# Two weight tiles split inside the opening of a hybrid decoder block, and two gate tiles moved ahead of the compression tiles

## The chip, the cores and the metric

One core of a Trainium2 chip runs the whole program. The metric is the device time of one execution in microseconds (us), as the median of several runs. The names of the engines are those of the profile: PE (TensorE, matrix products), DVE (VectorE), ACT (ScalarE), POOL (GpSimd) and SP (SyncE, which here issues nearly all loads).

## The reference, cut to what matters

The program computes one decoder layer on 512 tokens of width 1024. The input is normed, modulated, and projected by one wide matrix; its columns feed three token mixers (A, B and C) and three gates.

```python
ada = (cond @ ada_w[l] + ada_b[l])[:, None, :]
sh1, sc1, gt1, sh2, sc2, gt2 = jnp.split(ada, 6, axis=-1)
h = modulate(rmsnorm(x, norm1_w[l]), sh1, sc1)
p = h @ w_in[l]
p_a, p_b, p_c, p_gate = split_cols(p, IN_GROUPS)
y_a = hgrn2_mixer(*split_cols(p_a, A_SPLITS), ...)      # gated linear recurrence
y_b = nsa_mixer(*split_cols(p_b, B_SPLITS), ...)        # compressed / selected / window attention
y_c = rwkv7_mixer(p_c, ...)                             # delta rule; p_c is first mixed with its shifted self
ga, gb, gc = jnp.split(jax.nn.sigmoid(p_gate), 3, axis=-1)
merged = ga * (y_a @ w_branch[l, 0]) + gb * (y_b @ w_branch[l, 1]) + gc * (y_c @ w_branch[l, 2])
x = x + gt1 * (merged @ w_out[l])
h = modulate(rmsnorm(x, norm2_w[l]), sh2, sc2)
x = x + gt2 * ((jax.nn.silu(h @ ffn_w1[l]) * (h @ ffn_w3[l])) @ ffn_w2[l])
return rmsnorm(x, final_norm_w)
```

## The kernel before

Every large product is made in three matrix products of reduced-precision halves. A weight tile (128 columns of `w_in`, 128x1024 floats in the buffer `wraw`, of which there are three) is loaded by SP. ACT casts it to its high half `whi`, DVE subtracts to get its low half `wlo` (two buffers each), and PE then multiplies `whi` with `hhi`, `whi` with `hlo` and `wlo` with `hhi` for each of eight slices of the inner dimension, 24 matmuls in all, into an accumulator of a ring. The rings are called "g", "f", "m" and "n" and have two accumulators each; the trace names the products by the ring.

The opening is scheduled by the compiler's own list scheduler. `first_gemm` (line 579) makes the modulated input `h` slice by slice and multiplies each slice at once with six column tiles of mixer C, whose accumulators are two of "m", "g" and "f". The loop of line 608 takes the six in the order 0 to 5. Then `c_setup` (line 723) reads the six accumulators through `c_shift`: ACT scales, DVE adds the row shifted by one token. It begins with the two "m" accumulators (`lora` and `xg`, with a tanh and a sigmoid), then takes the "g" and "f" ones, which frees them.

From line 1614 on comes the counted phase (`manual_schedule`): instructions keep the order in which the program emits them, and the program picks that order by counting estimated times. `order.job` is the list of weight tiles; `order.chain` adds the mixers' step chains ("C", "pre", "A"), the conditioning sums ("D") and the bias table ("bias"). The function `tend` (line 292) loads up to three tiles ahead and splits only the first of the list, and only when all that it needs is done. `Weights` is one tile with its load, its split and its steps. The first two of the list are the query and the forget tile of head 0 of mixer A (`af("q", 0)`, `af("f", 0)`). Towards the end of the list stand eight compression tiles `kt` of mixer B, whose raw weights are used unsplit (they hold a `wraw` buffer until their products have run), and eight gate tiles `gt`. These write `merged`, which lies in the pool `pm`; that pool is opened when chain "A" is through. After the compression tiles the chain "K" (`b_compress`) makes the compressed keys and values in small steps; the attention's preparation and `b_mixer` follow, with the branch products as filling work for PE.

In the listing, `self.bproj` holds the query buffer "bq" from the start. `b_bias` (line 1213) uses it for a row of its table, and `yc` and `ya` are the two "y" buffers for the outputs of mixers C and A.

Of the kernel before, what the change touches and what calls it, by code (L numbers as in the profile page):

```python
# [17 lines left out]
P = 128  # L18
T = 512
D = 1024  # L20
KT = 8
# [82 lines left out]
class Clock:  # L104


    def __init__(self):
        self.at = dict.fromkeys(("PE", "DVE", "ACT", "POOL", "SP"), 0.0)
        self.wrote, self.read, self.slots, self.seen, self.by = {}, {}, {}, {}, {}
        self.bus, self.func, self.last, self.held = 0.0, None, 0.0, 0.0  # L110
# [97 lines left out]
class Order:  # L208
# [83 lines left out]
    def tend(self):  # L292

        loaded = sum(w.raw is not None and (w.w is None or w.split is None) for w in self.tiles)
        loaded += bool(self.steps and self.tile.split is None)
        for x, w in enumerate(self.tiles[:4]):
            if w.raw is None:
                if loaded >= 3:
                    break
                w.prepare(self.clock, 0)  # L300
                loaded += 1

        for x, w in enumerate(self.tiles[:3]):
            if all(n in self.done for n in w.needs):
                if x and self.tiles[0].hi is None:
                    self.tiles.insert(0, self.tiles.pop(x))
                break
        if self.tiles and all(n in self.done for n in self.tiles[0].needs):
            self.tiles[0].prepare(self.clock, 1)

    def job_ready(self):
# [43 lines left out]
class Weights:  # L355


    def __init__(self, load, split, steps, needs=(), ring="g"):
        self.load, self.split, self.todo, self.needs, self.ring = load, split, steps, needs, ring
        self.raw = self.w = self.hi = None  # L360

    def prepare(self, clock, split):
# [22 lines left out]
class Trunk:  # L385
# [193 lines left out]
    def first_gemm(self, xs, pool):  # L579

        nc, V = self.nc, self.nc.vector
        h = self.h
        s1 = self.t(self.cp, [P, 8], "s1")
        offs = (1536, 1664, 512, 640, 0, 1024)
        pss = [self.psm(), self.psm(), self.psg(), self.psf(), self.psg(), self.psf()]
        pa, px = self.psn(), self.psn()

        def ada(k):
            if k not in self.first_a:
                return  # L590
            aw, n = self.first_a[k]
            acc = self.t(pool, [P, 2, 2, P], "facc", bufs=2)[:, :, :n]
            for kk in range(KT):
                self.ada_sum(acc, kk, aw[:, :, kk])
            for x in range(n):
                self.ada_cols(pa[:, 2 * (k + x):2 * (k + x) + 2], [acc[:, 0, x], acc[:, 1, x]], k + x, 8)
            V.scalar_tensor_tensor(s1[:, k:k + n], self.adaT[:, 8 + k:8 + k + n], 1.0, self.vec("norm1_w", k, n), op0=ALU.add, op1=ALU.mult)

        def products(ks):
            w = []  # L600
            for k in ks:
                raw = self.first_w[k]
                whi = self.t(self.wp, [P, 1024], "whi", F32R, bufs=2)
                wlo = self.t(self.wp, [P, 1024], "wlo", F32R, bufs=2)
                nc.scalar.copy(whi[:, :768], raw[:, :768])
                V.tensor_tensor(wlo[:, :768], raw[:, :768], whi[:, :768].bitcast(F32), op=ALU.subtract)
                w.append((whi, wlo))
            for q in range(6):
                qs = slice(q * P, (q + 1) * P)
                for k, (whi, wlo) in zip(ks, w):  # L610
                    self.mm3(pss[q], (whi[:, qs], wlo[:, qs]), (h[0][:, k], h[1][:, k]), k == 0, k == KT - 1)

        ada(0)
        ada(1)
        self.modulate(xs, 0, px, h, s1[:, 0:1], self.adaT[:, 0:1], pool)
        for k in range(KT):
            if k + 2 < KT:
                ada(k + 2)
            if k + 1 < KT:
                self.modulate(xs, k + 1, px, h, s1[:, k + 1:k + 2], self.adaT[:, k + 1:k + 2], pool)  # L620
            if k != KT - 2:
                products((k,) if k < KT - 1 else (k - 1, k))
        return h, dict(zip(offs, pss))
# [73 lines left out]
        nc.vector.tensor_tensor(lo[:, :f], raw[:, :f], hi[:, :f].bitcast(F32), op=ALU.subtract)  # L697
        return tuple(x[:, :f].rearrange("p (k n) -> p k n", k=nk) for x in (hi, lo))

    def full(self, src, h, end, needs=()):  # L700

        st = []

        def steps(w):
            def step(k):
                if k == 0:
                    st.append(self.psg())
                self.mm3(st[0], (w[0][:, k], w[1][:, k]), (h[0][:, k], h[1][:, k]), k == 0, k == KT - 1)
                if k == KT - 1:
                    end(st[0])  # L710

            return [lambda k=k: step(k) for k in range(KT)]

        return Weights(lambda: self.load_w(src, KT, P), lambda raw, hi: self.cut_w(raw, hi, KT, P), steps, needs)

    def proj(self, off, h, tag, n=128):
        ps = self.psum(tag)
# [5 lines left out]
    def c_setup(self, first):  # L723

        nc = self.nc
        self.ck = {}
        lora = self.lora = self.c_shift(first.pop(1536), 12, "lora")
        nc.scalar.activation(lora[:64], lora[:64], AF.Tanh)
        xg = self.xg = self.c_shift(first.pop(1664), 13, "xg")
        nc.scalar.activation(xg, xg, AF.Sigmoid)  # L730
        for off, j, tag, bufs in ((512, 4, "k", 2), (0, 0, "r", 1), (1024, 8, "v", 2), (640, 5, "k", 2)):
            self.ck[off] = self.c_shift(first.pop(off), j, tag, bufs)

    def c_shift(self, ps, j, tag, bufs=1):
        nc = self.nc
# [398 lines left out]
    def a_mixer(self, y):  # L1134
# [3 lines left out]
        for hd in range(4):  # L1138
# [66 lines left out]
            for i in range(4):  # L1205
                tr(ps[:, i * P:(i + 1) * P], yo[:, i], self.ident)
            nw = self.vec("hgrn_norm_w", hd)
            nc.scalar.activation(y[:, hd], ps, AF.Identity, scale=nw)
            done[f"A{hd}"] = self.order.at
            yield "now"  # L1210


    def b_bias(self, qT, vg):

        nc = self.nc
        vg, qT = (x.rearrange("p a b -> p (a b)") for x in (vg, qT))
        rb, oh, row = vg[:33, TOEP:TOEP + 8], vg[:33, :TOEP], qT[:8, :TOEP]
        nc.gpsimd.memset(rb, NEG)
        nc.sync.dma_start(rb[:32], self.i["rel_bias"])
        nc.sync.dma_start(oh, self.i["onehot"])  # L1220
        yield rb, oh, ":n"
        for c0, n in ((0, 512), (512, TOEP - 512)):
            ps = self.psn()
            self.mm(ps[:8, :n], rb, oh[:, c0:c0 + n], start=True, stop=True)
            nc.vector.tensor_copy(row[:, c0:c0 + n], ps[:8, :n])
        yield row
        d = self.t(self.dr, [8, TOEP], "toep8")
        nc.sync.dma_start(d, row)
        yield 20.0
        self.b_spread(d)  # L1230
# [7 lines left out]
    def b_tiles(self, h):  # L1238
# [11 lines left out]
            return self.full(w_in[:, B_OFF + off:B_OFF + off + 128], h, end)  # L1250


        qT = self.t(pool, [P, 4, T], "bq")

        def query(i):
            src = [w_in[:, B_OFF + 256 * g + 64 * i:B_OFF + 256 * g + 64 * i + 64] for g in range(2)]
            return self.full(src, h, lambda ps: nc.scalar.mul(qT[:, i], ps, 0.125))

        vg = self.t(pool, [P, 4, 280], "bvg")
        gt = self.t(pool, [P, 4, 24], "bgt")  # L1260
# [19 lines left out]

            return Weights(lambda: self.load_w(src, 2, 280), lambda raw, hi: self.cut_w(raw, hi, 2, 280), steps, (), None)

        self.bproj = qT, kT, vg, gt
        return {**{nm: key(nm, off) for nm, off in (("kc", 512), ("vc", 640), ("ks", 768), ("kw", 1024))},
                "q": [query(i) for i in range(4)], "v": [value(kq) for kq in range(4)]}

# [232 lines left out]
    def gate_tiles(self, b, h):  # L1519

        def tile(m):
            off = G_OFF + 1024 * b + 128 * m

            def end(ps):
                self.nc.scalar.activation(self.merged[:, m], ps, AF.Sigmoid)

            return self.full(self.i["w_in"][0, :, off:off + 128], h, end, ("pm",))

        return [tile(m) for m in range(8)]

# [33 lines left out]
    def run(self):  # L1564
# [10 lines left out]
        with tc.tile_pool(name="p0", bufs=1) as p0:  # L1575
# [29 lines left out]
            self.turn_vecs(vrows[0])  # L1605
            h, first = self.first_gemm(xs, p0)
            self.turn_vecs(vrows[1])
        self.pc = pcs.enter_context(tc.tile_pool(name="pc", bufs=1))
        with tc.using_default_side("right"):
            self.pa = pas.enter_context(tc.tile_pool(name="pa", bufs=1))  # L1610
        yc, ya = self.new_y(), self.new_y()
        order = self.order
        self.cp_, self.a_ = {}, {}
        with tc.manual_schedule():
# [6 lines left out]
            order.chain("D", self.ada_steps(), 5, None)  # L1621

            bt = self.b_tiles(h)
            order.chain("bias", self.b_bias(self.bproj[0], self.bproj[2]), 6, None)
            av = lambda n, *x: self.a_pair_tiles(A_OFF + 1024 + 256 * n, h, "av", AF.Identity, f"av{n}", x)
            sg = lambda n, *x: self.a_pair_tiles(A_OFF + 1536 + 256 * n, h, "asg", AF.Sigmoid, f"sg{n}", x)
            af = lambda nm, hd, *x: self.a_tile(nm, hd, h, x)
            cr = lambda nm, p, *x: self.c_tile(nm, p, h, x)
            order.job(af("q", 0), af("f", 0), *av(0), cr("r", 1, "b0"), cr("v", 1), *sg(0), af("q", 1, "qd0"), af("f", 1, "fd0"),
                      cr("k", 2, "g0"), bt["kc"], bt["vc"], af("q", 2, "qd1"), cr("r", 2, "b1"), cr("v", 2, "G0"), af("f", 2, "fd1"),  # L1630
                      *av(1, "A1"), *sg(1, "A1"), bt["ks"], af("q", 3, "qd2"), bt["kw"], cr("k", 3, "g1"), af("f", 3, "fd2"),
                      cr("r", 3, "b2"), cr("v", 3, "G1"), *bt["q"], *bt["v"])
            kt, gt = self.b_compress_tiles(), self.gate_tiles(0, h)
            order.job(*gt[:2], *[x for n in range(4) for x in (kt[2 * n], kt[2 * n + 1], gt[2 + n])], *gt[6:])
            order.run("A")
            self.dump("ya", ya)
            pas.close()
            pks = ExitStack()
# [189 lines left out]
```

## Time and profile before

| what | us |
|---|---|
| median of 3 runs | 1171.03 (1169.71 to 1173.94) |
| the profiled execution's own time | 1174.54 |
| its span, first to last instruction | 1172.6 |
| PE busy | 1120.2 |
| DVE busy | 656.4 |
| ACT busy | 412.0 |
| POOL busy | 82.7 |

The span is what the profile shows; the execution's own time has a little around it. Matmuls overlap in the profile, so a busy PE is not a PE at its peak; the pitch from start to start tells more than the duration of one. Times in the rows are counted from the span's start. The bracket at the end of a timeline row is the idle time of the engine before that instruction and what ended it.

### The profile page before, as it was taken

The page shows a single profiled execution, that of the slowest core. Times are in us where ns is not written, and L with a number is a line of the kernel's source. Part 1 is how long each engine was busy: PE and PEld are TensorE (multiplying, and loading weights), DVE is VectorE, ACT ScalarE, POOL GpSimd, SP SyncE. Part 2 cuts the span into 40 slices and gives each one's busy share as a digit, 9 for nine tenths or more (in the row PEclk, how much of TensorE's full clock was granted, in tenths as well). Part 3 has the DMA queues.
Part 4 walks back from the last instruction along what each step waited for, and adds up shares of the span by engine and source line. Part 5 has one row for each costly group of instructions (what it writes and reads, how often), then busy time and mean ns, then how long its engine had stood idle before and what let it go on. Part 6 is the DMA issues. An engine that isn't in the chain of part 4 may idle for free.

```text
span 1172.6 us, 18592 instructions
## 1 busy us (share of the span) xinstructions
PE 1120.2 (96%) x7497; PEld 912.0 (78%) x7497; DVE 656.4 (56%) x1396; ACT 412.0 (35%) x737; POOL 82.7 (7%) x96
## 2 busy tenths in 40 slices
PE   3989999999999999899999989998999999999997
PEld 3759887878887887577878758887888888888886
DVE  5858666666757766377666745446343343432533
ACT  4352421242332231155454654435232322322221
POOL 1001010120111000110112002110000000000000
PEclk9989999999999999889999999999999999999999
DMA  9934532324243244643222105542233333333231
GB/s 284 257 105 143 131 97 73 84 67 141 57 111 82 71 118 117 194 147 99 73 63 76 33 1 148 155 137 78 85 90 100 98 90 108 90 94 104 90 108 72
DMA packets 183086, 125.28 MB, mean 107 GB/s; under 512 B 27929, under 2 KB 163111, under 8 KB 183000
## 3 DMA queue, kind: packets, MB, share of 16 engines
q1 hardware_dynamic: 182424, 123.04, 37.0%
q8 instruction: 59, 0.97, 0.3%
q10 hardware_dynamic: 576, 1.05, 0.2%
q14 instruction: 27, 0.22, 0.1%
HBM read 121.15 MB, written 5.53 MB: 108 GB/s over the span
## 4 chain that ended last, share of the span: by engine, by line
PE 86%; DVE 4%; DMA 4%; SPq 2%; ACT 2%; issue 2%; POOL 0%; POOLq 0%; DVEq 0%; ACTq 0%
PE g L438 27%; PE f L438 27%; PE m L438 18%; PE n L438 11%; SPq L191 2%; PE n L442 2%; DMA adaw<-in_ada_w_dram 1%; DMA fw<-in_w_in_dram 1%; DMA wraw<-in_w_in_dram 1%; DVE wlo L191 1%; DMA x<-in_x_dram 1%; PE m L442 1%; ACT bpt L191 0%; DVE adacc L191 0%; DVE ylo L191 0%
## 5 line engine op out<-in xcount | busy, mean ns | idle before, releaser
L191 DVE TENSOR_TENSOR wlo<-wraw,whi 128x1024 fp32r<-128x1024 f32 (+2 forms) x144 | 164.1, 1139 | 158.3 <-ACT whi L191 156.5
L191 ACT CAST whi<-wraw 128x1024 fp32r<-128x1024 f32 (+2 forms) x144 | 139.1, 967 | 282.8 <-PE f L438 119.6
L438 PE MATMUL g<-hhi,whi 128*128 128x512 f32 x360 | 155.5, 432 | 9.6 <-ACT whi L191 9.6
L438 PE MATMUL g<-hhi,wlo 128*128 128x512 f32 x360 | 143.6, 399 | 1.9 <-DVE wlo L191 1.8
L438 PE MATMUL g<-hlo,whi 128*128 128x512 f32 x360 | 143.3, 398 | 0.0
L438 PEld LDWEIGHTS g<-hhi,whi 128*128 128x128 f32 x360 | 69.8, 194 | 29.5 <-ACT whi L191 10.9
L438 PE MATMUL f<-hhi,whi 128*128 128x512 f32 x232 | 91.8, 396 | 0.0
L438 PE MATMUL f<-hhi,wlo 128*128 128x512 f32 x232 | 90.9, 392 | 0.0
L438 PE MATMUL f<-hlo,whi 128*128 128x512 f32 x232 | 90.6, 390 | 0.0
L438 PEld LDWEIGHTS g<-hhi,wlo 128*128 128x128 f32 x360 | 69.0, 192 | 20.1 <-DVE wlo L191 4.7
L438 PEld LDWEIGHTS g<-hlo,whi 128*128 128x128 f32 x360 | 69.4, 193 | 11.4 <-issue 0.5
L191 DVE SCALAR_TENSOR_TENSOR adacc<-adaw,cond,adacc 128x512 f32<-128x512 f32 x56 | 42.5, 759 | 15.6 <-DMA adaw<-in_ada_w_dram 15.0
L438 PEld LDWEIGHTS f<-hhi,whi 128*128 128x128 f32 x232 | 44.3, 191 | 8.9
L438 PEld LDWEIGHTS f<-hhi,wlo 128*128 128x128 f32 x232 | 43.6, 188 | 9.0
L438 PEld LDWEIGHTS f<-hlo,whi 128*128 128x128 f32 x232 | 43.6, 188 | 8.5
L438 PE MATMUL f<-whi,hhi 128*128 128x256 f32 (+1 forms) x144 | 44.4, 308 | 0.0
L191 DVE CUSTOM_DVE_ANT_0 bs<-m,bW 128x128 f32<-128x128 f32 (+3 forms) x64 | 30.1, 486 | 24.5 <-PE m L438 15.3
L438 PE MATMUL f<-whi,hlo 128*128 128x256 f32 (+1 forms) x144 | 41.6, 289 | 0.0
L438 PE MATMUL f<-wlo,hhi 128*128 128x256 f32 (+1 forms) x144 | 41.5, 288 | 0.0
L438 PE MATMUL f<-yhi,whi 128*128 128x512 f32 x96 | 38.8, 404 | 2.2 <-ACT yhi L191 1.4
L191 ACT ACTIVATE bs<-bs,bst 128x128 f32<-128x128 f32 (+3 forms) x64 | 35.9, 563 | 12.9 <-DVE bst L191 12.4
L191 POOL TENSOR_TENSOR merged<-merged,msg 128x512 f32<-128x512 f32 x16 | 25.9, 1622 | 202.4 <-DVE msg L191 194.5
(439 smaller groups left out, 2376.8 us busy)
## 6 DMA issues: line engine op xcount, KB each, us to landing
wraw<-in_ffn_w_dram SPq DMA_DIRECT2D x66, 512.0 KB
wraw<-in_w_in_dram SPq DMA_DIRECT2D x52, 512.0 KB
adaw<-in_ada_w_dram SPq DMA_DIRECT2D x64, 256.0 KB
aw<-in_ada_w_dram SPq DMA_DIRECT2D x16, 512.0 KB
wraw<-in_w_branch_dram SPq DMA_DIRECT2D x16, 256.0 KB
wraw<-in_w_out_dram SPq DMA_DIRECT2D x8, 512.0 KB
fw<-in_w_in_dram SPq DMA_DIRECT2D x24, 128.0 KB
toep<-toep SPq DMA_DIRECT2D x8, 320.0 KB
```

The costliest lines, as they stand in the source:

```text
L191: r = f(*a, **kw)
L438: return self.nc.tensor.matmul(o, l, r, **kw)
L442: return self.nc.tensor.transpose(o, x, ident)
```

## The change

Two tiles are split in the opening. After `first_gemm` the program now loads and splits the first two tiles of the job list into `held`, with the query buffer "bq" and one "y" buffer as the place for their halves; the two `Weights` are handed these when the job list is made. The query buffer itself, the bias table's row and `ya` are therefore allocated later, and the bias chain first waits for the mark `qA0`, set when the first tile has ended. `first_gemm` takes the two "g" tiles first, and `c_setup` reads these two first. The flag `early` lets `tend` split the first gate tile before `pm` is open. In the job list four gate tiles, not two, stand ahead of the compression tiles, and after the last pair of them one gate is left instead of three.

```diff
-        if self.tiles and all(n in self.done for n in self.tiles[0].needs):
+        if self.tiles and (self.tiles[0].early or all(n in self.done for n in self.tiles[0].needs)):
             self.tiles[0].prepare(self.clock, 1)
...
-            for q in range(6):
+            for q in (2, 4, 0, 1, 3, 5):
...
-        lora = self.lora = self.c_shift(first.pop(1536), 12, "lora")
-        nc.scalar.activation(lora[:64], lora[:64], AF.Tanh)
-        xg = self.xg = self.c_shift(first.pop(1664), 13, "xg")
-        nc.scalar.activation(xg, xg, AF.Sigmoid)
-        for off, j, tag, bufs in ((512, 4, "k", 2), (0, 0, "r", 1), (1024, 8, "v", 2), (640, 5, "k", 2)):
-            self.ck[off] = self.c_shift(first.pop(off), j, tag, bufs)
+        for off, j, tag, bufs in ((512, 4, "k", 2), (0, 0, "r", 1), (1536, 12, "lora", 1), (1664, 13, "xg", 1), (640, 5, "k", 2), (1024, 8, "v", 2)):
+            o = self.ck[off] = self.c_shift(first.pop(off), j, tag, bufs)
+            if off == 1664:
+                lora, xg = self.lora, self.xg = self.ck.pop(1536), self.ck.pop(1664)
+                nc.scalar.activation(lora[:64], lora[:64], AF.Tanh)
+                nc.scalar.activation(xg, xg, AF.Sigmoid)
...
-            nc.scalar.activation(y[:, hd], ps, AF.Identity, scale=nw)
+            if hd == 0:
+                y.append(self.new_y())
+            nc.scalar.activation(y[0][:, hd], ps, AF.Identity, scale=nw)
...
-        rb, oh, row = vg[:33, TOEP:TOEP + 8], vg[:33, :TOEP], qT[:8, :TOEP]
+        vg = vg.rearrange("p a b -> p (a b)")
+        yield "qA0"
+        rb, oh, row = vg[:33, TOEP:TOEP + 8], vg[:33, :TOEP], self.t(self.pbr, [8, TOEP], "bq")
...
+                if i == 0:
+                    self.bproj[0] = self.t(pool, [P, 4, T], "bq")
+                nc.scalar.mul(self.bproj[0][:, i], ps, 0.125)
...
-            return self.full(self.i["w_in"][0, :, off:off + 128], h, end, ("pm",))
+            return self.full(self.i["w_in"][0, :, off:off + 128], h, end, ("pm",), m == 0)
...
+            held = []
+            with tc.using_default_side("right"):
+                where = self.t(self.pbr, [P, 2, 1024], "bq", F32R), self.t(self.yp, [P, 2, 1024], "y", F32R, bufs=2)
+            for off, dst in zip((A_OFF, A_OFF + 512), where):
+                held.append(self.split_w(i["w_in"][0, :, off:off + P], KT, P, (dst[:, 0], dst[:, 1])))
...
-            order.job(af("q", 0), af("f", 0), *av(0), cr("r", 1, "b0"), cr("v", 1), *sg(0), af("q", 1, "qd0"), af("f", 1, "fd0"),
+            first = af("q", 0), af("f", 0)
+            for x, w in zip(first, held):
+                x.raw, x.w = w[0], w
+            order.job(*first, *av(0), cr("r", 1, "b0"), cr("v", 1), *sg(0), af("q", 1, "qd0"), af("f", 1, "fd0"),
...
-            order.job(*gt[:2], *[x for n in range(4) for x in (kt[2 * n], kt[2 * n + 1], gt[2 + n])], *gt[6:])
+            order.job(*gt[:4], *[x for n in range(4) for x in (kt[2 * n], kt[2 * n + 1], gt[4 + n])])
```

## Rows read from the trace of the kernel before

**Rows 1.** The page: one engine's busy time (share, instructions), and one load's size.
```profile
PE 1120.2 (96%) x7497; PEld 912.0 (78%) x7497; DVE 656.4 (56%) x1396; ACT 412.0 (35%) x737; POOL 82.7 (7%) x96
...
wraw<-in_w_in_dram SPq DMA_DIRECT2D x52, 512.0 KB
```
**Rows 2.** PE's waits, whole span: us in total, times, longest.
```profile
PE g L438 <- ACT whi L191: 9.6, 3, 5.3
```
**Rows 3.** Windows at the opening's end, columns as in the first line.
```profile
core 0: us, PE busy (x) PEld busy (x) DVE busy (x) ACT busy (x) POOL busy (x), PEclk, DMA share, GB/s
66.60:71.90 5.30, 0.01 (x1) 0.01 (x1) 3.44 (x6) 4.48 (x8) 0.00 (x0) 0.71 0.00 0
71.90:76.10 4.20, 4.16 (x10) 2.59 (x11) 3.39 (x5) 0.88 (x1) 0.00 (x0) 0.56 0.38 116
```
**Rows 4.** Timeline of PE: start, duration, instruction, [idle before].
```profile
71.89 0.80 PE L438 MATMUL g<-hhi,whi 128*128 128x512 f32 x1 [5.34 <-ACT whi L191]
...
75.76 0.40 PE L438 MATMUL g<-hhi,wlo 128*128 128x512 f32 x1
76.09 1.24 PE L438 MATMUL n<-bvg 33*8 33x512 f32 x4
...
82.77 0.39 PE L438 MATMUL g<-hhi,whi 128*128 128x512 f32 x1
...
87.30 0.40 PE L438 MATMUL g<-hhi,wlo 128*128 128x512 f32 x1
```
**Rows 5.** Timeline of ACT from 60.
```profile
64.44 0.69 ACT L191 ACTIVATE lora<-m,omu 128x512 f32<-128x512 f32 x1 [4.65 <-PE m L438]
...
70.78 2.00 ACT L191 CAST whi<-wraw 128x1024 fp32r<-128x1024 f32 x2
```
**Rows 6.** Timeline of DVE from 60.
```profile
65.16 0.75 DVE L191 SCALAR_TENSOR_TENSOR lora<-m,vT,lora 128x511 f32<-128x511 f32 x1 [2.47 <-ACT lora L191]
...
71.87 1.23 DVE L191 TENSOR_TENSOR wlo<-wraw,whi 128x1024 fp32r<-128x1024 f32 x1
```
**Rows 7.** Windows of the compression stretch, columns as in rows 3.
```profile
472.90:476.30 3.40, 0.00 (x0) 0.00 (x0) 0.01 (x1) 1.04 (x1) 0.05 (x1) 0.81 0.45 122
476.30:481.90 5.60, 5.55 (x14) 4.04 (x15) 2.78 (x5) 0.00 (x0) 0.00 (x0) 0.51 1.04 305
...
498.80:502.30 3.50, 3.50 (x11) 2.59 (x10) 2.81 (x4) 1.22 (x2) 0.00 (x0) 0.51 0.97 283
...
519.60:522.50 2.90, 1.49 (x8) 0.91 (x8) 2.77 (x8) 2.86 (x6) 0.30 (x1) 1.00 0.00 0
```
**Rows 8.** Timeline of PE behind the last compression tile.
```profile
495.60 0.38 PE L438 MATMUL f<-wraw,msg 128*62 128x256 f32 x1
496.78 0.50 PE L438 MATMUL g<-hhi,whi 128*128 128x512 f32 x1 [0.80 <-ACT whi L191]
...
498.29 0.50 PE L438 MATMUL g<-hhi,wlo 128*128 128x512 f32 x1 [0.77 <-DVE wlo L191]
```
**Rows 9.** The chain of waits from 440 to 510: start, us, what.
```profile
470.08 5.11 DMA wraw<-in_w_in_dram
...
489.70 5.91 DMA wraw<-in_w_in_dram
```
**Rows 10.** Timeline of SP's DMA issues, the last of the opening.
```profile
51.82 4.76 SPq L191 DMA_DIRECT2D wraw<-in_w_in_dram  x3
```
**Rows 11.** Windows of the opening, columns as in rows 3.
```profile
58.00:60.00 2.00, 2.00 (x10) 1.64 (x9) 1.12 (x2) 1.40 (x2) 0.00 (x0) 1.00 0.96 286
60.00:62.00 2.00, 2.00 (x10) 1.37 (x9) 0.51 (x1) 0.00 (x0) 0.00 (x0) 1.00 0.04 13
```
**Rows 12.** Timeline of PE, the last products of chain "K".
```profile
506.17 0.86 PE L438 MATMUL n<-bw,e 128*128 128x64 f32 x6
```
**Rows 13.** Timeline of ACT in the opening, one of the last modulations.
```profile
55.54 0.78 ACT L191 ACTIVATE nh<-n,adaT,s 128x512 f32<-128x512 f32 x1 [2.67 <-DVE s L191]
```
**Rows 14.** Windows of the attention, columns as in rows 3.
```profile
650.00:660.00 10.00, 10.00 (x61) 8.01 (x61) 5.85 (x20) 5.92 (x15) 0.00 (x0) 1.00 0.24 62
660.00:670.00 10.00, 8.97 (x69) 6.02 (x67) 9.30 (x41) 7.39 (x20) 0.00 (x0) 1.00 0.06 16
```

More of the change, by code (lines that the diff above doesn't have):

```diff
@@ L355, with __init__ @@
 class Weights:
-    def __init__(self, load, split, steps, needs=(), ring="g"):
-        self.load, self.split, self.todo, self.needs, self.ring = load, split, steps, needs, ring
+    def __init__(self, load, split, steps, needs=(), ring="g", early=False):
+        self.load, self.split, self.todo, self.needs, self.ring, self.early = load, split, steps, needs, ring, early
         self.raw = self.w = self.hi = None
@@ L698, in cut_w, with full @@
         return tuple(x[:, :f].rearrange("p (k n) -> p k n", k=nk) for x in (hi, lo))
-    def full(self, src, h, end, needs=()):
+    def full(self, src, h, end, needs=(), early=False):
         st = []
@@ L712, in steps @@
             return [lambda k=k: step(k) for k in range(KT)]
-        return Weights(lambda: self.load_w(src, KT, P), lambda raw, hi: self.cut_w(raw, hi, KT, P), steps, needs)
+        return Weights(lambda: self.load_w(src, KT, P), lambda raw, hi: self.cut_w(raw, hi, KT, P), steps, needs, early=early)
     def proj(self, off, h, tag, n=128):
@@ L1207, in a_mixer, with b_bias @@
             nw = self.vec("hgrn_norm_w", hd)
-            nc.scalar.activation(y[:, hd], ps, AF.Identity, scale=nw)
+            if hd == 0:
+                y.append(self.new_y())
+            nc.scalar.activation(y[0][:, hd], ps, AF.Identity, scale=nw)
             done[f"A{hd}"] = self.order.at
             yield "now"
-    def b_bias(self, qT, vg):
+    def b_bias(self, vg):
         nc = self.nc
-        vg, qT = (x.rearrange("p a b -> p (a b)") for x in (vg, qT))
-        rb, oh, row = vg[:33, TOEP:TOEP + 8], vg[:33, :TOEP], qT[:8, :TOEP]
+        vg = vg.rearrange("p a b -> p (a b)")
+        yield "qA0"
+        rb, oh, row = vg[:33, TOEP:TOEP + 8], vg[:33, :TOEP], self.t(self.pbr, [8, TOEP], "bq")
         nc.gpsimd.memset(rb, NEG)
@@ L1250, in key, with end @@
             return self.full(w_in[:, B_OFF + off:B_OFF + off + 128], h, end)
-        qT = self.t(pool, [P, 4, T], "bq")
         def query(i):
             src = [w_in[:, B_OFF + 256 * g + 64 * i:B_OFF + 256 * g + 64 * i + 64] for g in range(2)]
-            return self.full(src, h, lambda ps: nc.scalar.mul(qT[:, i], ps, 0.125))
+            def end(ps):
+                if i == 0:
+                    self.bproj[0] = self.t(pool, [P, 4, T], "bq")
+                nc.scalar.mul(self.bproj[0][:, i], ps, 0.125)
+            return self.full(src, h, end)
         vg = self.t(pool, [P, 4, 280], "bvg")
@@ L1281, in value @@
             return Weights(lambda: self.load_w(src, 2, 280), lambda raw, hi: self.cut_w(raw, hi, 2, 280), steps, (), None)
-        self.bproj = qT, kT, vg, gt
+        self.bproj = [None, kT, vg, gt]
         return {**{nm: key(nm, off) for nm, off in (("kc", 512), ("vc", 640), ("ks", 768), ("kw", 1024))},
@@ L1610, in run @@
             self.pa = pas.enter_context(tc.tile_pool(name="pa", bufs=1))
-        yc, ya = self.new_y(), self.new_y()
+        yc, ya = self.new_y(), []
         order = self.order
@@ L1623, in run @@
             bt = self.b_tiles(h)
-            order.chain("bias", self.b_bias(self.bproj[0], self.bproj[2]), 6, None)
+            order.chain("bias", self.b_bias(self.bproj[2]), 6, None)
             av = lambda n, *x: self.a_pair_tiles(A_OFF + 1024 + 256 * n, h, "av", AF.Identity, f"av{n}", x)
@@ L1633, in run @@
             kt, gt = self.b_compress_tiles(), self.gate_tiles(0, h)
-            order.job(*gt[:2], *[x for n in range(4) for x in (kt[2 * n], kt[2 * n + 1], gt[2 + n])], *gt[6:])
+            order.job(*gt[:4], *[x for n in range(4) for x in (kt[2 * n], kt[2 * n + 1], gt[4 + n])])
             order.run("A")
+            ya = ya[0]
             self.dump("ya", ya)
```

## Prediction

> **What bounds the kernel now.** I read the page first: TensorE (PE) is busy 96% of the 1172.6 us span [rows 1]. So the end moves only with what takes idle or slow time from PE or adds PE work, and this change adds none. Next I read the list of PE's waits: "g" products waiting for the ACT cast of a weight tile to its high half (whi) lose 9.6 us in three waits, the longest 5.3 us [rows 2]. The windows and timelines then place them. The reader is to see two places.
>
> The opening's end. From 66.6 to 71.9 PE does 0.01 us of work, and then it runs at a mean granted clock of 0.56 until 76.1 [rows 3]. At the lower of its two levels (1.2 of 2.4 GHz), nine products take from 71.89 to 76.09; later, twenty go from 82.77 to 87.30, 0.2265 us each [rows 4]. ACT spends that idle time on the six token-shifts of `c_setup` and comes to the first counted cast only at 70.78 [rows 5]; DVE follows it [rows 6].
>
> The compression stretch. PE is idle 3.40 us before the fourth gate tile and then runs 5.6 us at clock 0.51; after the last compression tile it idles 0.80 and 0.77 and runs 3.5 us at 0.51 [rows 7, 8]. The releaser is a cast that waited for its load: 5.11 and 5.91 us from issue to landing, in the chain of waits [rows 9].
>
> **The opening, edit by edit.** The two loads of `held` stand where before issues its first three weight loads, at 51.82 behind the masks [rows 10]. In before, traffic runs at 286 GB/s from 58 to 60 and all but stops from 60 [rows 11]; so the third load has landed about 60, and at 512 KB (0.524 MB) each [rows 1] the second about 58.2 and the first about 56.4 (estimates from that row). The two casts cost 2.00 us on ACT [rows 5], which does nothing from 60 to 62 [rows 11] and waits for PE until 64.44 [rows 5]; the two subtractions cost 1.23 us each on DVE, which sits idle 2.47 us before its first shift at 65.16 [rows 6] and is busy 0.51 of the 2 us before 62 [rows 11]. So both tiles are split by about 64, hidden under `first_gemm`'s last products. No instruction is added: two casts, two subtractions, two loads move forward. The third load becomes that of the tile after them.
>
> A split tile still needs a free "g" accumulator. Putting those two columns first in `first_gemm` gives them the place that lora's had: ACT started on lora at 64.44 and DVE ended its shift at 65.16 + 0.75 = 65.91 [rows 5, 6]. With "k" now first in `c_setup`, the first accumulator is free by 65.9, before PE runs dry at 66.55; the second, one shift later, has a whole tile (24 x 0.2265 = 5.4 us) of cover. The shifts themselves are the same in number. Lora's shift comes two shifts later in ACT's order, but its first reader stands behind a whole tile of products.
>
> So the idle 5.34 us goes [rows 4]. PE then goes from products to products, and the slow nine go too: 76.09 - 71.89 = 4.20 against 9 x 0.2265 = 2.04, that is 2.16. Sum: **-7.5**. Lowest gain: the casts queued too early (a rival below); more than -7.5 there is not to take. The Trainium skill, "TensorE: Matmul & The Clock Gate", Part 1, has start to start N / 1.2 GHz, 426.7 ns, for such a product at the lower level and 215.7 at the higher. By these nine products would give 1.90 instead of 2.16, an estimate from that page, and the sum -7.2.
>
> The bias chain now waits for the first tile's end, because its row shares the buffer. Its four matmuls (1.24 us at 76.09 [rows 4]) run later, not longer; its two small loads pass behind the next weight loads on SP, and its table is read first hundreds of us later. The late allocation of the query and y buffers waits on readers that ended long before. Cost 0; without that cover it would be the 1.24 us, once.
>
> The early split of gate tile 0 has nothing to hide in this profile: the three waits of "g" for a cast add up to 9.6 us [rows 2], and 5.34, 3.40 and 0.80 at the places above use them up, so that tile waits for none. I take 0; it could gain only if the new order of the phase leaves the gate waiting.
>
> **The compression stretch, worked out.** Two gates (48 x 0.2265 = 10.9 us of PE) move from behind the compression tiles to ahead of them. In before the fourth gate's load could not be issued until 470.08, because unsplit compression tiles held the three raw buffers. With four gates leading, that tile is loaded and split before, and this junction goes: 3.40 idle plus 5.6 x (1 - 0.51) = 2.7 of slow clock, -6.1. But the pattern compression, compression, gate is then repeated three times without other PE work beside it, where before has it once at the end; two junctions are added. That one cost 0.80 + 0.77 idle [rows 8] and 3.5 x 0.49 = 1.7 of slow clock [rows 7]. Each added one costs nothing if its load lands under the gate before it, 6.1 if it is like the first. I take the nearest row, between its idle alone (1.57) and all of it (3.27): 2.4 each, +4.8. Net **-1.3**, bounds -6.1 and +6.1.
>
> Behind the last compression tile (its last matmul is at 495.60) the compression's own small steps run until 506.17 + 0.86 = 507.03 [rows 8, 12]: 11.4 us that two gates partly filled, with one more behind. Now one gate is left, 5.4 us. So between 0 and 6.0 us of PE can lie open, and the attention's preparation, which waits for those buffers, has less cover too. The nearest row is the junction where the last gate ended before the preparation did: 2.90 - 1.49 = 1.4 us idle [rows 7]. I take **+1.4**.
>
> **Sum.** -7.5 - 1.3 + 1.4 = -7.4. The profiled execution took 1174.54 (span 1172.6 and 1.94 around it), 3.5 above the median of the runs, 1171.03. So 1167.1 for such an execution, and 1163.6 at the median, -0.63%. About 0.5%, 5.9 us, is what a measurement tells from no change: faster below 1165.2, slower above 1176.9.
>
> **Rivals.**
> Loads hidden in every cycle: the junctions cost nothing, -7.5 - 6.1 + 1.4 = -12.2, 1158.8. For it: a cycle moves 1.57 MB in 7 us of PE, less than the 286 GB/s that traffic reaches. Against it: one load of 0.52 MB alone took 5.11 us [rows 9], and its issue waits for a buffer that the gate before it frees. The Trainium skill, "DMA: Bandwidth & Descriptors", Anatomy of one DMA, fits 2.0 us plus bytes at 436 GB/s, 3.2 us for 0.52 MB (an estimate from its fit for GpSimd's queue); by that rule this rival would be the likely one, and the trace's 5.11 us does not agree.
>
> Cycles dear, or the tail open: two junctions like the first give -7.5 + 6.1 + 1.4 = 0.0, 1171.0; the tail wholly open gives -7.5 - 1.3 + 6.0 = -2.8, 1168.2.
>
> The casts queue too early: ACT works in order. If the casts stand ahead of the modulation at 55.54 [rows 13], ACT waits for loads that land about 56.4 and 58.2; that modulation would come 2.0 us late with one cast ahead, 3.7 with both, and the products of that column and all behind them too: 1165.6 to 1167.3. Against it: the idle from 60 on lies right after the landing.
>
> Slower than before: the attention's chain decides, not PE. It can start only when the compression has ended. The last compression tile ends 10.9 later by two gates, 4.8 by two junctions, 6.1 earlier by the first, 7.5 by the opening: +2.1, 1173.1, and if the junctions cost 6.1 each, +9.5, 1180.5. It decides if PE's filling work is not what paces the attention. Against it: PE is full (10.00 of 10) while filling work lasts and DVE only 5.85; when the filler is used up at 660, DVE rises to 9.30 and PE loses just 1.0 in 10 [rows 14]. The chain gains speed when filler is gone.
>
> **Chances.** Forecast 0.50, own range 1160 to 1166.5; hidden loads 0.15; dear cycles or open tail 0.18; early casts 0.11; slower 0.06. The range 1157.5 to 1170.5 takes in both sides of the opening and the middle of the compression bounds, and leaves out some 0.16. Below 1165.2 lie four fifths of the forecast, the hidden loads and a little of the early casts, 0.58; above 1176.9 half of the slower case and a bit of chance, 0.04.
>
> **What would show it.** Right: the first "g" product within 0.5 us of the opening's last, the clock at 1.00 from 66 to 76, the two casts before 64.4, no 3.4 us idle before the fourth gate, and 1 to 3 us lost at each of the later junctions. Wrong: a modulation later than 55.5 or 58.4 in the opening; the 7.5 us back as idle between the first weight tiles; the attention starting no earlier than at 519.6; or an order of the whole counted phase that has changed enough to open waits nowhere in this trace.

## Result and the profile after

The changed kernel is slower: 1181.40 us median of 4 runs (1180.85 to 1183.83) beside 1170.37 of before, ratio 1.0085 [1.0062, 1.0108]. The forecast of 1163.6 us fails in its sign. The profiled span grows by 9.4 us, from 1172.6 to 1182.0, and PE's busy time by 4.9 [rows 1]. The page of after:

```profile
PE 1125.1 (95%) x7497; PEld 913.5 (77%) x7497; DVE 661.6 (56%) x1396; ACT 412.7 (35%) x737; POOL 82.8 (7%) x96
```

In the opening, ACT's timeline answers to [rows 5, 13]:

```profile
58.19 1.04 ACT L191 CAST bq<-wraw 128x1024 fp32r<-128x1024 f32 x1 [6.33 <-DMA wraw<-in_w_in_dram]
...
59.88 1.04 ACT L191 CAST y<-wraw 128x1024 fp32r<-128x1024 f32 x1
...
63.46 0.78 ACT L191 ACTIVATE nh<-n,adaT,s 128x512 f32<-128x512 f32 x1 [1.80 <-DVE s L191]
```

DVE's timeline:

```profile
59.26 1.23 DVE L191 TENSOR_TENSOR bq<-wraw,bq 128x1024 fp32r<-128x1024 f32 x1 [5.96 <-ACT bq L191]
60.41 0.48 DVE L191 SCALAR_TENSOR_TENSOR facc<-aw,cond,facc 128x256 f32<-128x256 f32 x1
...
61.74 1.22 DVE L191 TENSOR_TENSOR y<-wraw,y 128x1024 fp32r<-128x1024 f32 x1
```

The chain of waits, and PE's timeline, which answers to [rows 4]:

```profile
51.56 6.61 DMA wraw<-in_w_in_dram
```
```profile
63.93 1.01 PE L438 MATMUL n<-ones,facc 128*128 128x1 f32 x4 [7.20 <-DVE facc L191]
...
76.36 0.40 PE L438 MATMUL f<-hhi,wlo 128*128 128x512 f32 x1
76.60 0.39 PE L438 MATMUL g<-hhi,bq 128*128 128x512 f32 x1
```

PE's windows, columns as in [rows 3]:

```profile
60.00:64.00 4.00, 0.07 (x1) 0.07 (x1) 4.00 (x9) 2.20 (x3) 0.00 (x0) 0.57 0.48 135
64.00:70.00 6.00, 6.00 (x18) 4.79 (x19) 2.75 (x7) 2.25 (x4) 0.12 (x1) 0.50 0.10 24
```

The reader is to see an inversion. The list scheduler has put the two early casts ahead of the last modulations on ACT, and the two subtractions ahead of the last conditioning sums (`facc`) on DVE. ACT stands 6.33 us at a cast whose load lands at 58.17; DVE stands 5.96 us behind ACT; the sums stand behind DVE's subtraction; PE waits 7.20 us for them and then runs 6 us at half clock (a granted clock of 0.50). `first_gemm` ends at 76.76, 10.2 later than before. What was to be gained is there all the same: the first counted product follows at 76.60, where before PE waited 5.34 us [rows 4].

In the compression stretch, PE's timeline answers to [rows 8]:

```profile
491.95 0.50 PE L438 MATMUL g<-hhi,whi 128*128 128x512 f32 x1 [0.63 <-ACT whi L191]
493.52 0.50 PE L438 MATMUL g<-hhi,wlo 128*128 128x512 f32 x1 [0.84 <-DVE wlo L191]
502.29 0.50 PE L438 MATMUL g<-hhi,wlo 128*128 128x512 f32 x1 [0.79 <-DVE wlo L191]
...
514.81 0.66 PE L442 MATMUL n<-ident,e 128*128 128x128 f32 x2 [2.00 <-DVE e L191]
...
531.66 0.47 PE L438 MATMUL m<-bkhi,bqs 128*128 128x128 f32 x1 [3.81 <-DVE bqs L191]
```

PE's windows behind these two last waits:

```profile
515.00:520.00 5.00, 5.00 (x20) 3.61 (x20) 1.29 (x5) 1.10 (x3) 0.00 (x0) 0.50 0.27 64
530.00:535.00 5.00, 2.82 (x7) 1.87 (x8) 4.78 (x12) 4.38 (x8) 2.02 (x2) 0.66 0.00 0
```

The first junction's 3.40 us is gone, the later junctions cost under 1.5 us each, and the tail opens: 2.00 us in chain "K" and 3.81 before the attention's first product, with 6.1 us more lost to half clock between 514 and 540.

All kernels with several executions, each beside its own runs of before. "Pinned" means that the early casts and subtractions are held behind the last modulation, as told at e3. The ratio and its interval are not the quotient of the two medians, and the two ways of telling a difference can lie up to 2.3 us apart:

| kernel | median | before | ratio, 95% interval |
|---|---|---|---|
| e1: opening as changed, two gates lead | 1180.58 | 1172.98 | 1.0070 [1.0056, 1.0084] |
| e2: before, four gates lead | 1183.77 | 1172.98 | 1.0098 [1.0079, 1.0116] |
| e3: pinned, two gates | 1170.79 | 1172.98 | 0.9979 [0.9964, 0.9994] |
| e4: pinned, four gates | 1171.83 | 1172.98 | 0.9993 [0.9981, 1.0005] |
| e5: loads early, two gates | 1176.01 | 1172.49 | 1.0025 [1.0008, 1.0041] |
| e6: before, new column order | 1188.00 | 1172.49 | 1.0120 [1.0083, 1.0158] |
| e9: pinned, three gates | 1169.41 | 1172.49 | 0.9969 [0.9952, 0.9986] |
| e11: pinned, order of before, two gates | 1165.32 | 1172.92 | 0.9919 [0.9890, 0.9948] |
| e12: pinned, order of before, four gates | 1174.57 | 1172.92 | 1.0010 [0.9992, 1.0028] |
| e13: pinned, order of before, three gates | 1164.76 | 1172.92 | 0.9923 [0.9894, 0.9951] |
| e14: only DVE pinned, two gates | 1178.27 | 1172.27 | 1.0032 [1.0009, 1.0056] |

Where a profiled execution lost PE time, in us: PE's idle time plus busy time x (1 - granted clock), summed over windows of 2 us.

| kernel | 40 to 100 | 100 to 240 | 240 to 310 | 310 to 450 | 450 to 545 | 650 to 840 |
|---|---|---|---|---|---|---|
| before | 8.3 | 2.2 | 3.9 | 0.9 | 12.6 | 10.2 |
| after | 11.5 | 0.8 | 6.6 | 1.8 | 15.4 | 9.7 |
| e2 | 8.6 | 2.2 | 1.9 | 0.9 | 20.1 | 9.8 |
| e3 | 0.9 | 0.8 | 4.3 | 1.4 | 11.9 | 8.6 |
| e10, e3 once more | 1.7 | 0.8 | 5.5 | 1.4 | 11.8 | 8.6 |
| e4 | 1.1 | 0.8 | 4.2 | 1.5 | 12.9 | 10.3 |
| e6 | 7.6 | 0.8 | 9.9 | 5.1 | 18.4 | 8.7 |
| e9 | 1.7 | 0.8 | 5.7 | 1.4 | 11.4 | 9.6 |
| e11 | 1.6 | 3.2 | 5.6 | 0.9 | 13.4 | 10.2 |
| e12 | 1.3 | 3.2 | 3.0 | 0.9 | 22.3 | 9.8 |
| e13 | 1.3 | 1.5 | 0.7 | 1.0 | 10.3 | 9.6 |

The sum over 545 to 650 is 0 in all of them.

### The profile page after: what moved, and what is told of

Same layout as the page of the kernel before. It is cut to its first block, busy times and chain, and to the rows that moved or that the text cites. A ratio compares the mean times of both kernels' runs of the same rounds, so it can differ in the third digit from the quotient of the medians.

```text
span 1182.0 us, 18592 instructions
## 1 busy us (share of the span) xinstructions
PE 1125.1 (95%) x7497; PEld 913.5 (77%) x7497; DVE 661.6 (56%) x1396; ACT 412.7 (35%) x737; POOL 82.8 (7%) x96
## 4 chain that ended last, share of the span: by engine, by line
PE 86%; DVE 6%; DMA 3%; SPq 2%; issue 1%; ACT 1%; POOL 0%; POOLq 0%; DVEq 0%; ACTq 0%
PE f L438 28%; PE g L438 26%; PE m L438 18%; PE n L438 11%; SPq L191 2%; PE n L442 2%; DMA fw<-in_w_in_dram 1%; DMA x<-in_x_dram 1%; DMA adaw<-in_ada_w_dram 1%; PE m L442 1%; DVE wlo L191 1%; DMA wraw<-in_w_in_dram 1%; DVE y L191 0%; ACT bpt L191 0%; DVE bs L191 0%
## 5 line engine op out<-in xcount | busy, mean ns | idle before, releaser
L191 DVE TENSOR_TENSOR wlo<-wraw,whi 128x1024 fp32r<-128x1024 f32 (+2 forms) x142 | 166.2, 1171 | 150.2 <-ACT whi L191 149.8
L438 PE MATMUL g<-hhi,whi 128*128 128x512 f32 x344 | 148.8, 436 | 0.7 <-ACT whi L191 0.6
L438 PE MATMUL g<-hhi,wlo 128*128 128x512 f32 x344 | 137.1, 398 | 2.2 <-DVE wlo L191 2.2
L438 PE MATMUL g<-hlo,whi 128*128 128x512 f32 x344 | 136.7, 397 | 0.0
L438 PEld LDWEIGHTS g<-hhi,whi 128*128 128x128 f32 x344 | 65.2, 191 | 21.3 <-issue 6.2
L438 PEld LDWEIGHTS g<-hhi,wlo 128*128 128x128 f32 x344 | 65.7, 191 | 18.9 <-DVE wlo L191 4.3
L438 PEld LDWEIGHTS g<-hlo,whi 128*128 128x128 f32 x344 | 66.0, 192 | 11.4 <-issue 1.2
L438 PE MATMUL f<-yhi,wlo 128*128 128x512 f32 x96 | 39.1, 407 | 0.5 <-DVE wlo L191 0.5
```

The source lines that it names most:

```text
L191: r = f(*a, **kw)
L438: return self.nc.tensor.matmul(o, l, r, **kw)
```

## Experiments

Theory A: the casts stand too early in ACT's queue, and that costs some 10 us. Theory B: four leading gates leave the compression's small steps and the attention's start without cover. Their rivals: the loss comes from the other half of the change alone, or from what the counting makes of it behind (theory C, formed at e6).

**e1 and e2: one half of the change each.**

```diff
# e1: the changed kernel with
-            order.job(*gt[:4], *[x for n in range(4) for x in (kt[2 * n], kt[2 * n + 1], gt[4 + n])])
+            order.job(*gt[:2], *[x for n in range(4) for x in (kt[2 * n], kt[2 * n + 1], gt[2 + n])], *gt[6:])
# e2: the kernel before with the reverse
```

> The changed kernel with the gate tiles back in their old order (two lead, three behind). Theory A with B (the casts of the two early tiles stand ahead of the last modulations on ACT and wait there for a load, about 10 us late, against 7.5 us gained behind; the four leading gates cost some 7 us of their own): opening as in the changed kernel, first junction idle again, end at 1171 to 1175 us. Rival (the opening makes all of the loss): 1179 to 1183 us. Rival (the gates make all of it): 1168 to 1171 us.

> The kernel before with nothing but the new order of the gate tiles, four ahead. Theory B (the two gates that no longer stand behind the compression tiles leave the compression's small steps and the attention's start without cover; more than the first junction gives back): 1175 to 1180 us, first junction without idle time, PE idle and half clock behind the last compression tile. Rival (the gates do what was predicted, the loss is the opening's): 1164 to 1170 us.

The opening alone is 1.0070, nearly all of the loss: more than the 1171 to 1175 of theory A. The gates alone are 1.0098, also all of it, and more than the 1175 to 1180 that theory B gave them. Nor did they do what theory B expected: the first junction did not go. PE's timeline of e2:

```profile
489.89 0.79 PE L438 MATMUL g<-hhi,whi 128*128 128x512 f32 x1 [4.32 <-ACT whi L191]
```

Two halves that each cost the whole (7.6 and 10.8 us by the medians, 11.0 together) do not add up, so something is shared or differs between them; e11 and e12 show what.

**e3 and e4: the casts held behind the last modulation.** `last_h` is the last cast and the last subtraction of `modulate`, and `issue_after` queues what follows on their engines behind them. Nothing else of the change is touched: the counted phase keeps the order of e1 in e3 and that of the changed kernel in e4.

```diff
+            with tc.issue_after(self.last_h[0]), tc.issue_after(self.last_h[1]):
                 for off, dst in zip((A_OFF, A_OFF + 512), where):
                     held.append(self.split_w(i["w_in"][0, :, off:off + P], KT, P, (dst[:, 0], dst[:, 1])))
```

> The changed kernel with the two casts issued behind the last modulation on ACT and the two subtractions behind the last one on DVE, and the gate tiles in their old order. Theory A: the modulations are back at 55.5 and 58.4 us, first_gemm ends near 66.2, the first counted product follows at once, and the end comes 7.5 us earlier than before: 1161 to 1165 us. Rival (the place in the queue is not what costs; the early tiles' loads or the new planner order do): 1169 us or more.

> As the pinned kernel with two gates leading, but with four gates leading, as in the change. Theory B: 6 to 9 us slower than with two gates, 1168 to 1173 us. Rival (with a clean opening the gates gain as predicted): 0 to 6 us faster than with two gates, 1157 to 1163 us.

ACT's timeline of e3, then its first counted product on PE and a window of PE:

```profile
57.87 0.78 ACT L191 ACTIVATE nh<-n,adaT,s 128x512 f32<-128x512 f32 x1 [0.65 <-DVE s L191]
...
59.21 1.05 ACT L191 CAST bq<-wraw 128x1024 fp32r<-128x1024 f32 x1
60.16 1.04 ACT L191 CAST y<-wraw 128x1024 fp32r<-128x1024 f32 x1
```
```profile
65.87 0.39 PE L438 MATMUL g<-hhi,bq 128*128 128x512 f32 x1
```
```profile
64.00:70.00 6.00, 6.00 (x27) 4.86 (x27) 4.09 (x7) 4.75 (x8) 0.00 (x0) 1.00 0.72 227
```

The casts lie in the idle time that the prediction had named, and PE has neither idle time nor half clock there; e3 loses 0.9 us between 40 and 100 where before lost 8.3. The place in the queue costs 12.2 us by the medians of the changed kernel and e4 (+11.0 against -1.2, each from its own before) and 9.8 by those of e1 and e3, which share their runs of before: what theory A says of the queue is shown. Its time is not. e3 gains 2.2 us in the medians, not 7.4, and lies in the range of the rival that named the new order; e11 parts the two. Four gates cost 1.0 over two, neither the 6 to 9 of theory B nor the gain of its rival.

**e5 and e14: the wait, and which queue.** In e5 the two loads go out ahead of the vectors, constants and masks; in e14 only the subtractions are held.

```diff
# e5
+            early = [self.load_w(i["w_in"][0, :, off:off + P], KT, P) for off in (A_OFF, A_OFF + 512)]
             vrows[1] = self.load_vecs(1, p0)
# e14
-            with tc.issue_after(self.last_h[0]), tc.issue_after(self.last_h[1]):
+            with tc.issue_after(self.last_h[1]):
```

> The changed kernel with two gates leading, not pinned, but the loads of the two early tiles are issued ahead of the small vector loads, the constants and the masks, some 6 us earlier, so that the casts find their data. If the wait for the load is what costs (theory A): the casts wait for little, the last modulation is within 2 us of 58.4, and the end is 2 us or less behind the pinned kernel of 1170.8: 1169 to 1173 us. Rival (the time of the casts and subtractions themselves, in front of the last modulations and sums, is what costs): 1176 us or more.

> As the pinned kernel with two gates leading, but only the subtractions on DVE are held behind the last one of the opening; the casts on ACT stand ahead of the last modulations as in the change. If the casts in ACT's queue are what delays (theory A as first put): ACT waits to 58.2 again, the slice's own cast behind it comes near 59, DVE's sums behind that, and the end is 1176 to 1181 us. If the subtractions in DVE's queue, which hold up the conditioning sums, are what delays: 1169 to 1173 us, as with both held (1170.8).

ACT of e5, and ACT, DVE and PE of e14:

```profile
51.34 1.04 ACT L191 CAST bq<-wraw 128x1024 fp32r<-128x1024 f32 x1 [3.97 <-DMA wraw<-in_w_in_dram]
```
```profile
57.80 1.04 ACT L191 CAST bq<-wraw 128x1024 fp32r<-128x1024 f32 x1 [5.97 <-DMA wraw<-in_w_in_dram]
```
```profile
59.60 0.96 DVE L191 TENSOR_TENSOR wlo<-fw,whi 128x768 fp32r<-128x768 f32 x1 [5.81 <-ACT whi L191]
```
```profile
61.53 1.01 PE L438 MATMUL n<-ones,facc 128*128 128x1 f32 x4 [4.78 <-DVE facc L191]
```

In e5 the loads land earlier but still late; the cast waits 3.97 us, and the kernel lies between the pinned one and e1 (medians against before: -2.2, +3.5, +7.6, with waits of 0, 3.97 and 5.46). Its 1176.0 is at the lower edge of what the rival expected. It does not part the wait from the casts' own time cleanly, since its second and later modulations are pushed as well. e14 is at +6.0, as expected of ACT's queue: the casts on ACT alone bring 8.2 of the 9.8 by the medians (6.2 of 10.7 by the ratios), because the slice's own cast stands behind them and DVE's subtraction and sums behind that. ACT's queue is the main cause, and DVE's hands it on; how much of the remainder the subtractions cost by themselves is not shown.

**e6 and e10: where the rest of the gain went.** e6 is the kernel before with only the new order of columns and shifts; e10 is e3 once more.

> The kernel before with only the new order of the columns in first_gemm and of the shifts in c_setup, no tile split early, gates as before. The pinned kernel kept 7.4 us of the opening in its profile but only 2.2 us in the medians. If the new order that the counting picks for the phase behind costs the rest: 1174 to 1178 us (before 1173.0 in that comparison). Rival (the order costs nothing; the pinned kernel's other executions lose clock at places that vary): within 2 us of before.

> The pinned kernel with two gates once more, for a second profiled execution: the first took 1166.8 at a mean clock of 0.993, the median of twelve is 1170.8 at 0.987. If the difference lies in half-clock stretches that come and go: the same order and the same idle times, and an additional stretch of half clock of several us somewhere in the counted phase or behind the attention. Rival: a wait that the first profile did not have.

e6 is 1.0120, far more than I gave it: no tile is split early, and it loses 15.5 us. Its table row shows the loss behind the opening, 6.0 us more than before between 240 and 310, 4.2 to 450 and 5.8 to 545. The counting sees the shifts end at other times, picks another order for the whole phase, and that one is worse. e10 took 1169.6, 2.8 more than the profiled execution of e3, with nearly the same idle times. What it has more is half clock, 1.7 us between 80 and 100 and 1.4 between 240 and 310. Windows of the first place, e3 first:

```profile
80.00:100.00 20.00, 20.00 (x188) 19.33 (x187) 19.28 (x35) 7.04 (x11) 7.39 (x6) 1.00 0.29 81
```
```profile
80.00:100.00 20.00, 20.00 (x154) 19.78 (x155) 17.76 (x31) 7.35 (x11) 7.39 (x6) 0.91 0.28 81
```

**e11: the new opening with the old order behind it.** The counting is given the old sequence of shifts, and for the two early tiles a `load` and a `split` that only count and hand over what lies there; the bias row moves into other partitions of its own buffer, so that its chain starts as before. Behind the opening the issue order of PE and ACT is that of before.

```diff
+            order.clock.count = lambda *x: calls.append(x)
             self.c_setup(first)
+            order.clock.count = count
+            for n in (4, 5, 8, 6, 7, 9, 0, 1, 2, 3, 12, 13, 10, 11):
+                count(*calls[n])
...
+                x.load, x.split = load, split
...
-        yield "qA0"
-        rb, oh, row = vg[:33, TOEP:TOEP + 8], vg[:33, :TOEP], self.t(self.pbr, [8, TOEP], "bq")
+        rb, oh, row = vg[:33, TOEP:TOEP + 8], vg[:33, :TOEP], vg[64:72, :TOEP]
```

> The pinned kernel with two gates leading, but the counting is told the times of the old opening, and the bias row has a place of its own, so that the counted phase keeps the order of the kernel before instruction for instruction; only the opening differs. Theory C (the opening gains its 7.4 us; the new order that the counting picks behind it gives some 5 of them back): 6 to 8 us faster than before, ratio 0.993 to 0.995. Rival (the medians lose the gain to stretches of half clock that the shift in time itself brings, whatever the order): 2 us faster, as the pinned kernel was.

It is 7.6 us faster than before in the medians, ratio 0.9919 [0.9890, 0.9948], a little more than the 0.993 to 0.995 expected: theory C. The opening's gain is what the prediction worked out, and the new order, together with the later start of the bias chain, takes 5.4 us of it away (-7.6 against -2.2, each from its own before).

**e9, e12 and e13: how many gates lead.**

> As the pinned kernel, with three gate tiles leading and two behind the last compression tiles. Two leading gave 1170.8, four 1171.8. If the first junction's idle and the cover behind are traded against each other evenly (theory B, weak form): 1170 to 1172. If there is a best point between: 1168 or less.

> The kernel with the order of before and the early tiles pinned, with four gates leading: the same edit of the gates as in the kernel with four gates alone, which was 1.0098 of before, now on a clean opening. If the four gates cost what they cost there, whatever the opening: 10 us more than with two gates. Rival (they cost 1 us, as in the pinned kernel with the new order): 1 us more than with two gates.

> The same with three gates leading. In the pinned kernel with the new order three gates gave 1169.4 beside 1170.8 with two. Theory B's weak form: within 2 us of two gates. If the cover behind the compression decides: between two and four gates, some 5 us more than with two.

With the old order four gates cost 9.3 us over two, much as without the new opening (10.8); three cost nothing. With the new order three are 1.4 us faster than two, between what the two expectations of e9 had. PE's timeline of e12:

```profile
485.42 0.80 PE L438 MATMUL g<-hhi,whi 128*128 128x512 f32 x1 [5.00 <-ACT whi L191]
...
525.81 0.47 PE L438 MATMUL m<-bkhi,bqs 128*128 128x128 f32 x1 [3.80 <-DVE bqs L191]
```

and of e13:

```profile
510.18 0.33 PE L438 MATMUL m<-bkhi,bqs 128*128 128x128 f32 x1 [1.21 <-DVE bqs L191]
```

In the old order the first four compression tiles run in a row whatever leads, and the gate behind them waits 5.00 us for its cast; the junction that the change was to remove is still there, and the tail opens by 3.80. With four gates in the new order they run two by two, the junction goes, and the tail's loss is nearly balanced. So the same edit costs 9 us or 1 by the order around it, which is why e1 and e2 do not add up. The pair e9 and e13 has three gates each and differs in the order only. PE of e9, timeline and windows:

```profile
247.61 0.33 PE L438 MATMUL m<-XT,N 64*64 64x64 f32 x4 [0.58 <-DVE XT L191]
...
251.21 1.86 PE L438 MATMUL n<-ones,aq 128*128 128x1 f32 x8 [1.25 <-POOL aq L191]
```
```profile
250.00:255.00 5.00, 3.79 (x20) 3.66 (x20) 4.93 (x6) 1.58 (x2) 2.78 (x4) 0.62 0.00 0
255.00:260.00 5.00, 5.00 (x33) 4.80 (x33) 5.00 (x10) 0.00 (x0) 0.00 (x0) 0.70 0.39 108
```

and of e13:

```profile
250.00:255.00 5.00, 5.00 (x113) 4.48 (x112) 3.92 (x7) 2.60 (x4) 0.64 (x1) 1.00 0.01 3
```

The new order has two waits 3.6 us apart in the mixers' small steps near 250, and stretches of half clock with them; of the 6.6 us between the two spans (1167.9 and 1161.3), 5.0 lie between 240 and 310. The changed kernel has the same pair of waits at 256 and 260.

## Why the prediction was wrong

**The early splits, 0 predicted, about +10 to +12 measured.** This is the step that failed: "both tiles are split by about 64, hidden under `first_gemm`'s last products". Split they were, by 62.96 (61.74 + 1.22), but not hidden. The idle time was where it said (e3 uses it), but nothing put the casts there: the argument against the rival said where the casts fit, not where the scheduler puts them. The rival "the casts queue too early" was the mechanism, given 0.11 and 2.0 to 3.7 us. Three things were left out of its price. The first load landed at 58.17, not about 56.4: 6.61 us from issue. This is the least of the three: in e1 the cast began at 56.96, and the place in the queue cost nearly the same (10.7 by the ratios of e1 and e3, beside 10.8). The slice's own casts stood behind the early ones, and DVE's sums behind those, so the modulation of 55.54 [rows 13] came at 63.46, 7.9 late. And 7.20 us without products was followed by 6 us at clock 0.50, another 3.0. 7.2 + 3.0 is the 10.2 by which `first_gemm` ended late. That an instruction waiting at the head of ACT's or DVE's queue holds up all behind it is what these timelines show. The Trainium skill, "DMA: Bandwidth & Descriptors", Anatomy of one DMA, has a fit made for GpSimd's queue, by which that load would have landed near 54.8, an estimate; this trace does not agree. The Trainium skill, "PSUM — Partial Sum Buffer", Engine vs sequencer instructions, says that the queues of these two engines are strict FIFO, first in, first out; the trace agrees, with 6.33 us on ACT and 5.96 on DVE.

**The junction behind the opening, -7.5: right.** e11 measures -7.6 by the medians and -9.5 by the ratio, with an interval from -12.9 to -6.1, so the mechanism holds and the last tenth is luck. Every kernel with the tiles split has its first counted product straight behind `first_gemm`.

**The rest of the opening, 0 predicted, +5.4 measured.** "The shifts themselves are the same in number" held, but their order is an input of the counting. The prediction named a changed order as a thing that would make it wrong and gave it no price; e6 shows that it can be 15. That the bias chain starts later is part of this term; it was not tried alone.

**The compression stretch and the tail, -1.3 and +1.4: right in the sum, wrong in the parts.** With the order that the change has, four gates cost 1.0 over two (e4 against e3), and 0.1 was predicted. That is luck. In the changed kernel the first junction went as predicted, but the three others cost only 1.47, 0.79 and 0.34 us of idle time and no half clock, where 2.4 was taken for each of two added ones and 3.27 stood for the third; and the tail lost 2.00 + 3.81 us of idle time and 6.1 to half clock, where 1.4 was taken and 6.0 was the bound, which left out the clock. In the windows of e3 and e4 the junctions gave about 5 us and the tail took about 6. With the order of before the same edit is 9.3. Only the two bounds together (6.1 and 6.0) would hold that, and both took it for granted that the first junction goes. That the attention starts late (519.63 to 531.66) is this tail and the opening; behind it PE loses nothing between 545 and 650, so no chain paces it there.

**The early split of gate tile 0: exactly 0.** With the flag in e2, or without it in e3 or in the changed kernel, no instruction of PE, ACT, DVE or SP changes its place.

The sum of the steps, by medians against before: -7.6 (e11), +5.4 (e3), +1.0 (e4), +12.2 (changed kernel) is +11.0. By the ratios it is -9.5, +7.0, +1.6, +10.8, together +9.9. Each step is the difference of two kernels in a row, so the sum closes by construction and proves nothing by itself. e11 and e13 beat both kernels.

Left open: why the executions of e5 and e3 spread over 5 us. Of e5 one execution has a trace; the two of e3 (e10 is the second) differ by 2.6 us of span, in half clock and not in waits.

## What to carry to other kernels

An instruction that is moved into an idle stretch must be held there: ask what the scheduler will put behind it on its in-order engine, when its data land, and which other engine hands the delay on. Where a program plans its order from counted times, a small change at the start is also a new order behind it; keep the old order to measure the edit, then choose the order on its own merits. An edit of that order, such as the number of leading gates, has no price of its own apart from the order that it stands in.

## What the runs showed of the hardware

Half clock can come behind the same instructions in one execution and not in another. e11 and e13 run the same instructions in the same order there, and both have a 0.99 us wait in the same place. In e11 the granted clock is 1.00 until about 242, through 64 products of 64x64 behind the wait, then 0.50 until about 252; in e13 it is 1.00 throughout. PE's timeline and window of e11, then of e13:

```profile
239.55 0.50 PE L438 MATMUL g<-hhi,wlo 128*128 128x512 f32 x1 [0.99 <-DVE wlo L191]
```
```profile
245.00:250.00 5.00, 5.00 (x21) 3.39 (x20) 2.25 (x4) 2.90 (x3) 2.08 (x1) 0.50 0.00 0
```
```profile
237.75 0.50 PE L438 MATMUL g<-hhi,wlo 128*128 128x512 f32 x1 [0.99 <-DVE wlo L191]
```
```profile
245.00:250.00 5.00, 5.00 (x32) 3.66 (x31) 3.62 (x8) 0.30 (x1) 1.13 (x2) 1.00 0.53 157
```

That is 5.1 us of half clock in one execution (240 to 310) and none in the other. Nor is a wait needed. In e10 the profile shows PE without any wait from 80 to 100 (20.00 of 20), and yet the clock falls to 0.50 behind 24 products with few columns; in e3, the same kernel, it stays at 1.00 behind the same products. PE's timeline and window of e10, then the window of e3:

```profile
83.97 0.95 PE L438 MATMUL m<-consts,e 128*128 128x2 f32 x8
84.78 1.03 PE L438 MATMUL n<-ones,aq 128*128 128x1 f32 x8
85.67 1.08 PE L438 MATMUL n<-aqq,ak 128*128 128x64 f32 x8
```
```profile
88.00:90.00 2.00, 2.00 (x12) 2.00 (x11) 0.78 (x3) 0.00 (x0) 0.00 (x0) 0.50 0.67 229
```
```profile
88.00:90.00 2.00, 2.00 (x19) 2.00 (x19) 1.67 (x5) 0.79 (x1) 0.00 (x0) 1.00 0.54 181
```

So whether the wait or the small products behind it brought the half clock of e11 is not shown. The profiled execution of e11 was its slowest (1170.1 at a mean clock of 0.985; its others 1161.0 to 1165.8 at 0.988 to 0.993). A single profile cannot tell what a short wait costs; it takes the times of several executions, with the place of the wait.
